# Seven half-size products for a pair of up-projection tiles in an encoder's gated MLP

## The chip, the cores and the metric

The kernel runs on one core of one Trainium2 chip. The metric is the device time of one execution in microseconds (us). The core has a matrix engine (PE, TensorE), a vector engine (DVE), a scalar or activation engine (ACT), a general engine (POOL, GpSimd), and a queue engine (SP) that here only issues transfers. SBUF is the on-chip working memory that all of them read; PSUM holds matmul results, which PE writes and DVE and ACT read. The engines run their own instruction lists strictly in order and wait for each other through semaphores.

## The reference: a two-layer encoder, and its gated MLP

`x` has 512 rows of 1024 features. Each of the two layers applies a three-branch mixer (windowed attention, dense attention, spatial gating), a cross-attention into 256 memory rows, and a gated MLP, each followed by a residual and a layer norm. The change touches the MLP:

```python
def conv_ffn(x, w_up, conv_k, conv_b, w_down):
    S = x.shape[1]
    h = x @ w_up                                  # 512 x 1024 times 1024 x 5632
    r = CONV_W // 2
    hp = jnp.pad(h, ((0, 0), (r, r), (0, 0)))
    h = sum(hp[:, j:j + S] * conv_k[j] for j in range(CONV_W)) + conv_b
    a, b = jnp.split(h, 2, axis=-1)
    return (jax.nn.gelu(a, approximate=False) * b) @ w_down   # 2816 -> 1024
```

The up-projection gives 5632 features, 44 tiles of 128. Tile j (of a) and tile 22 + j (of b) make pair j; a convolution of width 3 along the rows, a GELU and a product turn a pair into tile j of g, and g times `w_down` follows.

## The kernel before

**Numbers.** Every fp32 operand is split into a high part, rounded to the matrix engine's fp32r type by ACT (`split_hi`, L127), and a low part, the rest, by DVE (`split_lo`, L132; a few weight tiles name POOL instead). A product is three matmuls (`mm3`, L138 to L140): high by high, high by low, low by high, added in PSUM.

**Weights.** All weights stream from HBM in chunks of 128 x 1024. `Weights.load` sends a chunk into one of two `raw` tiles; `Weights.split` makes the tile `w` (high and low) in one of six slots. `pump` splits the next chunk as soon as the step that used a slot last has been written, so the splits run up to six chunks ahead.

**Order.** `layer` appends `Step`s to a list, and a scheduler places each step's instructions on the engines by its own timeline. Only SP's order is written out by hand.

**The MLP.** When the layer norm of a row block is done, `xT_step` transposes it on PE and splits it into `xT` (features on partitions; high and low). Pairs 0 and 1 are computed in halves of 256 rows (`up_half_step`), the first halves before the last row blocks have arrived. Then `up_step(j, part)` runs for pairs 2 to 21 and both parts: 8 blocks of 128 input features by three matmuls of 128 x 512, 24 matmuls to a step, into an `acc` bank. `up_post` then does the convolution, straight from that bank (`conv`: an ACT instruction into `cv`, L124, and two SCALAR_TENSOR_TENSOR on DVE, L856 and L858), GELU on ACT for part 0, and for part 1 the product on POOL (L870) and the split of `g` on ACT and DVE. The down-projection follows: 11 `down_k_step`s for each half of the output columns (24 matmuls to a step), the last four chunks of the second half taken row block by row block in `down_t_step`.

Of the kernel before, what the change touches and what calls it, by code (L numbers as in the profile page):

```python
# [16 lines left out]
P = 128  # L17
# [56 lines left out]
def encoder_kernel(ctx: ExitStack, tc: tile.TileContext, x_in, xt_in, mem_in, w_in, pp_in, ln_in, cln_in, ws_in, co_in, out):  # L74
# [66 lines left out]


    class Weights:
        def __init__(self):
            self.order, self.pos, self.last = [], {}, []
            self.raw, self.tiles = {}, {}
            self.nl = self.ns = 0

        def plan(self, steps):
            for i, st in enumerate(steps):  # L150
                for key in st.chunks:
                    if key not in self.pos:
                        self.pos[key] = len(self.order)
                        self.order.append(key)
                        self.last.append(i)
                    else:
                        self.last[self.pos[key]] = i

        def load(self):
            j = self.nl  # L160
            r = wpool.tile([P, 1024], F32, tag="raw", name="raw", bufs=N_RAW)
            l, kind, c = self.order[j]
            nc.sync.dma_start(out=r, in_=w_in[l * NCH + CHUNK_ID[kind, c]])
            self.raw[j] = r
            self.nl += 1

        def split(self):
            j = self.ns
            while self.nl <= j:
                self.load()  # L170
            t = wpool.tile([P, 2, 1024], F32R, tag="w", name="w")
            r = self.raw.pop(j)
            split_hi(t[:, 0, :], r)
            l, kind, c = self.order[j]
            split_lo(t[:, 1, :], r, t[:, 0, :], eng=nc.gpsimd if (kind, c) in POOL_LO else nc.vector)
            self.tiles[j] = t
            self.ns += 1

        def pump(self, step):
            while self.ns < len(self.order) and (self.ns < N_WSLOT or self.last[self.ns - N_WSLOT] <= step):  # L180
                self.split()
            while self.nl < len(self.order) and self.nl < self.ns + N_RAW:
                self.load()

        def get(self, key, kk, n):
# [32 lines left out]

    def xT_step(t):
# [65 lines left out]
    def layer(l):  # L285
# [555 lines left out]

        def g_slot(j):
            if j % 4 == 0 and j < 20:
                R["g", j // 4] = big_tile([P, 4, 2, S], F32R, "g")
            elif j == 20:
                R["g", 5] = kv_p.tile([P, 2, 2, S], F32R, tag="k", name="g5")
            return g_view(j)

        def g_view(j):
            return R["g", j // 4][:, j % 4]  # L850

# [10 lines left out]
        def up_post(j, part, ps):  # L862
# [4 lines left out]
            else:  # L867
                c = conv(NPAIR + j, ps)
                ca = R.pop(("ca", j))
                nc.gpsimd.tensor_tensor(out=c, in0=ca, in1=c, op=ALU.mult)  # L870
# [4 lines left out]
        def up_step(j, part):  # L875
            key = K("up", part * NPAIR + j)

            def fn():
                ps = acc_tile()
                proj_fm(ps, key)  # L880
                pump()
                up_post(j, part, ps)
            return Step(fn, [key])

# [13 lines left out]
        def down_mm(half, c, t, ps):  # L898
            w = W.get(K("down", half * 11 + c), 2, 512)
            sl = slice(t * P, (t + 1) * P)  # L900
            for j in range(2):
                k = 2 * c + j
                g = g_view(k)
                mm3(ps, g[:, 0, sl], g[:, 1, sl], w[:, 0, j, :], w[:, 1, j, :], k == 0, k == 2 * 11 - 1)
# [330 lines left out]
```

## Time and profile before

| | |
|---|---|
| runs, us | 1821.01, 1822.25, 1822.78; median 1822.25 |
| profiled execution, us | 1821.99 |
| its span, us (first to last instruction) | 1820.2 |
| granted TensorE clock, mean | 0.994 |
| busy, share of the span | PE 98%, PE weight load 83%, DVE 58%, ACT 42%, POOL 17% |
| HBM traffic | 96 GB/s over the span |
| up-projection of layer 0, pairs 2 to 21 | about 572 to 789 us of the span |

Times in the profile are us from the span's start. A group's row gives the line, engine, operation, the names written and read, the shape, the count, then busy time and mean ns of one, then the engine's idle time ahead of them and what ended it. A timeline's row gives start, duration, engine, line and operation; where neighbours are merged ("x2") the duration is that of all of them together. Matmuls are pipelined, so the distance between the starts of two neighbours, and not the duration of one, is what a matmul costs in a stream.

### The profile page before, as it was taken

To read this page: it belongs to the slowest core of one execution; us is meant where nothing else is said; L and a number is where in the kernel's file an instruction comes from. 1 tells how busy PE (TensorE), PEld (TensorE's weight loads), DVE (VectorE), ACT (ScalarE), POOL (GpSimd) and SP (SyncE) were. 2 spreads that over 40 slices of the span, in tenths; PEclk is the share of its full clock that TensorE was granted. 3 is DMA by queue.
4 is the path that set the end of the run, shared out by engine and by line. 5 is a ranking of instruction groups with operands and counts; after the bars stand their busy time and mean duration, and the time that the engine had idled before them with its cause. 6 is when DMAs were issued, how large, how long until landed. Compare 5 with 4: busy or idle time off the path is not lost.

```text
span 1820.2 us, 23541 instructions
## 1 busy us (share of the span) xinstructions
PE 1789.6 (98%) x9064; PEld 1518.3 (83%) x9064; DVE 1064.8 (58%) x1728; ACT 755.7 (42%) x1274; POOL 317.2 (17%) x320
## 2 busy tenths in 40 slices
PE   8999999999999999999999999999999999999998
PEld 6888988878979888888888888888789788888886
DVE  6566856557676555543466568565576755555334
ACT  4346645532444444431133565455325344444210
POOL 1112422221131111100011124331201311111000
PEclk9999999999999999999999999999999999999999
DMA  6221221232422322332233222212334222232331
GB/s 220 91 84 64 82 93 58 74 126 93 161 70 93 102 95 93 104 115 95 91 133 106 80 70 84 79 59 82 130 105 136 82 89 97 93 104 93 107 102 46
DMA packets 51232, 176.60 MB, mean 97 GB/s; under 512 B 5680, under 2 KB 6192, under 8 KB 50864
## 3 DMA queue, kind: packets, MB, share of 16 engines
q1 hardware_dynamic: 44784, 158.86, 26.4%
q10 hardware_dynamic: 6336, 16.23, 2.6%
q8 instruction: 72, 1.18, 0.3%
q14 instruction: 40, 0.33, 0.1%
HBM read 170.87 MB, written 4.19 MB: 96 GB/s over the span
## 4 chain that ended last, share of the span: by engine, by line
PE 97%; DVE 1%; ACT 1%; DMA 0%; issue 0%; DVEq 0%; SPq 0%
PE acc L138 26%; PE acc L139 26%; PE acc L140 25%; PE s L567 2%; PE pv L604 1%; PE t L590 1%; PE s L139 1%; PE s L138 1%; PE s L140 1%; PE t L139 1%; PE t L138 1%; PE t L140 1%; PE pv L139 1%; PE pv L549 1%; PE s L483 1%; PE pv L138 1%
## 5 line engine op out<-in xcount | busy, mean ns | idle before, releaser
L132 DVE TENSOR_TENSOR w<-raw,w 128x1024 fp32r<-128x1024 f32 x284 | 354.5, 1249 | 438.5 <-ACT w L127 437.7
L127 ACT ACTIVATE w<-raw 128x1024 fp32r<-128x1024 f32 x292 | 309.2, 1059 | 481.7 <-PE acc L140 259.2
L138 PE MATMUL acc<-xT,w 128*128 128x512 f32 (+1 forms) x1216 | 457.5, 378 | 4.2 <-DVE x L234 4.2
L140 PE MATMUL acc<-xT,w 128*128 128x512 f32 (+1 forms) x1216 | 459.2, 378 | 0.0
L139 PE MATMUL acc<-xT,w 128*128 128x512 f32 (+1 forms) x1216 | 457.4, 377 | 0.0
L138 PEld LDWEIGHTS acc<-xT,w 128*128 128x128 f32 x1216 | 228.6, 189 | 44.2 <-DVE x L234 4.6
L139 PEld LDWEIGHTS acc<-xT,w 128*128 128x128 f32 x1216 | 229.6, 189 | 40.0
L140 PEld LDWEIGHTS acc<-xT,w 128*128 128x128 f32 x1216 | 229.5, 189 | 39.4
L138 PE MATMUL acc<-w,xT 128*128 128x512 f32 (+1 forms) x384 | 137.1, 359 | 7.1 <-ACT w L127 7.1
L139 PE MATMUL acc<-w,xT 128*128 128x512 f32 (+1 forms) x384 | 137.6, 358 | 1.2 <-DVE w L132 1.2
L140 PE MATMUL acc<-w,xT 128*128 128x512 f32 (+1 forms) x384 | 137.2, 357 | 0.0
L870 POOL TENSOR_TENSOR cv<-cv 128x512 f32<-128x512 f32 x44 | 57.0, 1296 | 431.9 <-DVE cv L858 389.1
L199 POOL TENSOR_TENSOR rs<-ve,mhalf 128x1 f32<-128x1 f32 x32 | 30.2, 943 | 421.6 <-DVE ve L244 371.2
L138 PEld LDWEIGHTS acc<-w,xT 128*128 128x128 f32 x384 | 73.0, 190 | 17.0 <-ACT w L127 7.3
L139 PEld LDWEIGHTS acc<-w,xT 128*128 128x128 f32 x384 | 73.0, 190 | 12.2 <-DVE w L132 2.0
L140 PEld LDWEIGHTS acc<-w,xT 128*128 128x128 f32 x384 | 73.1, 190 | 9.6
L502 POOL TENSOR_SCALAR ring<-ring,rsm 128x256 f32<-128x256 f32 (+1 forms) x64 | 43.9, 698 | 183.6 <-DVE rsm L500 107.0
L569 DVE TENSOR_REDUCE nm<-s 128x1 f32<-128x512 f32 x64 | 43.9, 689 | 52.0 <-PE s L567 51.4
L124 ACT ACTIVATE ring<-s,nm 128x512 f32<-128x512 f32 x64 | 44.0, 688 | 68.3 <-PE t L590 44.6
L655 POOL TENSOR_TENSOR mg<-mg,ring 128x512 f32<-128x512 f32 x32 | 47.8, 1495 | 138.6 <-DVE ring L654 111.1
L576 POOL TENSOR_SCALAR ring<-ring,rsm 128x512 f32<-128x512 f32 x64 | 45.9, 731 | 127.7 <-DVE rsm L574 127.7
L124 ACT ACTIVATE cv<-acc,pp 128x512 f32<-128x512 f32 x86 | 65.4, 761 | 1.6 <-PE acc L140 1.6
(237 smaller groups left out, 3303.5 us busy)
## 6 DMA issues: line engine op xcount, KB each, us to landing
raw<-in_w_dram SPq DMA_DIRECT2D x292, 512.0 KB, 3.4
lngb<-in_ln_dram ACTq DMA_DIRECT2D x16, 256.0 KB, 4.4
xraw<-in_xt_dram SPq DMA_DIRECT2D x4, 512.0 KB, 4.8
memr<-in_mem_dram ACTq DMA_DIRECT2D x2, 1024.0 KB, 4.7
x<-in_x_dram ACTq DMA_DIRECT2D x4, 512.0 KB, 5.8
x_keep<-x ACTq DMA_DIRECT2D x4, 512.0 KB, 2.6
x<-x_keep ACTq DMA_DIRECT2D x4, 512.0 KB, 7.7
out_dram<-x SPq DMA_DIRECT2D x8, 256.0 KB, 2.0
```

Of the source, the lines that this page charges most:

```text
L124: return nc.scalar.activation(out, in_, func, **kw)
L127: nc.scalar.activation(out, in_, AF.Copy, scale=scale)
L132: eng.tensor_tensor(out=out, in0=in_, in1=hi.bitcast(F32), op=ALU.subtract)
L138: nc.tensor.matmul(ps, lhsT=lh, rhs=rh, start=first, stop=False)
L139: nc.tensor.matmul(ps, lhsT=lh, rhs=rl, start=False, stop=False)
L140: nc.tensor.matmul(ps, lhsT=ll, rhs=rh, start=False, stop=last)
L502: nc.gpsimd.tensor_scalar(out=pr_t[qi], in0=pr_t[qi], scalar1=rs[:, qi:qi + 1], scalar2=0.0, op0=ALU.mult, op1=ALU.add)
L567: nc.tensor.matmul(ps, lhsT=R["Q"][:, h, q * P:(q + 1) * P], rhs=R["Kt"][:, kv * 2 + hl, :], start=hl == 0, stop=hl == 1)
L569: nc.vector.tensor_reduce(out=nm[:, qi:qi + 1], in_=ps, axis=AX.X, op=ALU.max, negate=True)
L576: nc.gpsimd.tensor_scalar(out=pr_t[qi], in0=pr_t[qi], scalar1=rs[:, qi:qi + 1], scalar2=0.0, op0=ALU.mult, op1=ALU.add)
L655: nc.gpsimd.tensor_tensor(out=mg, in0=mg, in1=tg, op=ALU.add)
L870: nc.gpsimd.tensor_tensor(out=c, in0=ca, in1=c, op=ALU.mult)
```

## The change

Pair j, for j from 2 to 21, is now computed by `up7_steps`. The 512 x 1024 input is cut into four blocks, A11 (rows 0 to 255, first 512 features), A12 (the same rows, last 512 features), A21 and A22 (rows 256 to 511); the pair's two weight tiles are cut into B11 and B21 (tile j, the first and last 512 input features) and B12 and B22 (tile 22 + j). Winograd's form of Strassen's method needs seven block products, each of 4 blocks of 128 features by three matmuls of 128 x 256, in place of eight. Two of the seven share the first of four steps (`s0`), two the second (`s1`), two the third (`s2`) and one the last (`s3`).

The sums of input blocks are made once to a layer (`sums_step`): four subtractions or additions on POOL of 128 x 1024, split by ACT and DVE into `S31` and `S24`. For that, `xT_step` also writes the unsplit transposed block (`xf`) by one more ACT copy for each of its two halves. The sums of weight blocks are made for every pair in `split_sums`: four additions of 128 x 512 on POOL, with their results split in four parts ("us" chunks, parts 0 to 3, of 1024, 1024, 1024 and 512 columns) on ACT and DVE. The seven products are put together into a new SBUF tile `h7` by three ACT copies and five DVE additions or subtractions of 128 x 256; `up_post` then runs from `h7` and no longer from PSUM. The split of `g` moves from `up_post` into the first half of the down-projection (`gs_make`), for which `g` is kept unsplit. There are five `w` slots in place of six and four `raw` tiles in place of two. The down-projection uses other PSUM banks.

```diff
-N_WSLOT = 6
-N_RAW = 2
+N_WSLOT = 5
+N_RAW = 4
...
+        def split_sums(self, t, l, c):
+            j, i = divmod(c, US_PARTS)
+            ra, rb = self.raw.get((l, "up", j)), self.raw.get((l, "up", NPAIR + j))
+            lo, hi = slice(0, 512), slice(512, 1024)
+            if i == 0:
+                split_hi(t[:, 0, :], ra)
+                split_lo(t[:, 1, :], ra, t[:, 0, :])
+            elif i == 1:
+                u = kv_p.tile([P, 512], F32, tag="k", name="usum")
+                nc.gpsimd.tensor_tensor(out=u, in0=ra[:, lo], in1=rb[:, lo], op=ALU.add)
+                nc.gpsimd.tensor_tensor(out=rb[:, lo], in0=rb[:, lo], in1=rb[:, hi], op=ALU.add)
+                for sl, r in ((lo, rb[:, lo]), (hi, u)):
+                    split_hi(t[:, 0, sl], r)
+                    split_lo(t[:, 1, sl], r, t[:, 0, sl])
+            elif i == 2:
+                nc.gpsimd.tensor_tensor(out=ra[:, lo], in0=ra[:, lo], in1=rb[:, lo], op=ALU.add)
+                nc.gpsimd.tensor_tensor(out=ra[:, hi], in0=ra[:, hi], in1=ra[:, lo], op=ALU.add)
+                split_hi(t[:, 0, :], ra)
+                split_lo(t[:, 1, :], ra, t[:, 0, :])
+            else:
+                split_hi(t[:, 0, lo], rb[:, hi])
+                split_lo(t[:, 1, lo], rb[:, hi], t[:, 0, lo])
...
                 evac_T(xT[:, t, 0, 4 * i:4 * i + 4, :], xT[:, t, 1, 4 * i:4 * i + 4, :], pt)
+                if plain is not None:
+                    act(plain()[:, 4 * i:4 * i + 4, t * P:(t + 1) * P], pt, AF.Copy)
...
+        def gs_make(k):
+            g, v = g_view(k), gs_view(k)
+            split_hi(v[:, 0, :], g)
+            split_lo(v[:, 1, :], g, v[:, 0, :])
...
-                nc.gpsimd.tensor_tensor(out=c, in0=ca, in1=c, op=ALU.mult)
-                g = g_slot(j)
-                split_hi(g[:, 0, :], c)
-                split_lo(g[:, 1, :], c, g[:, 0, :])
+                nc.gpsimd.tensor_tensor(out=g_view(j), in0=ca, in1=c, op=ALU.mult)
...
+        def sums_step():
...
+                nc.gpsimd.tensor_tensor(out=a22, in0=a21, in1=a22, op=ALU.subtract)
+                nc.gpsimd.tensor_tensor(out=a21, in0=a11, in1=a21, op=ALU.subtract)
+                put(R["S31"][:, 0], a21)
+                put(R["S31"][:, 1], a22)
+                nc.gpsimd.tensor_tensor(out=a11, in0=a22, in1=a11, op=ALU.subtract)
+                put(R["S24"][:, 0], a11)
+                nc.gpsimd.tensor_tensor(out=a12, in0=a12, in1=a11, op=ALU.add)
+                put(R["S24"][:, 1], a12)
...
+            def s1():
+                cd, h = R["p7", j][1], R["h7", j]
+                product(cd[:, lo], 1, 0, summed("S31", 0), True, False)
+                product(cd[:, hi], 1, 1, summed("S31", 1), False, True)
+                act(h[:, 1, hi], cd[:, lo], AF.Copy)
+                nc.vector.tensor_tensor(out=h[:, 1, hi], in0=cd[:, hi], in1=h[:, 1, hi], op=ALU.subtract)
+                pump()
...
+            def s3():
+                (ab, cd), h = R.pop(("p7", j)), R.pop(("h7", j))
+                product(cd[:, hi], 3, 0, summed("S24", 1), False, True)
+                nc.vector.tensor_tensor(out=h[:, 0, hi], in0=cd[:, lo], in1=h[:, 1, lo], op=ALU.add)
+                nc.vector.tensor_tensor(out=h[:, 1, lo], in0=cd[:, hi], in1=h[:, 1, lo], op=ALU.subtract)
+                pump()
+                up_post(j, 0, h[:, 0])
+                up_post(j, 1, h[:, 1])
...
         for j in range(2, NPAIR):
-            for part in range(2):
-                st(up_step(j, part))
+            for s7 in up7_steps(j):
+                st(s7)
+        add(lambda: [gs_make(k) for k in range(2)])
```

How the change moves instructions shows on DVE and POOL. DVE in the middle of the up-projection before: the seven instructions of one pair (`w` is a weight tile's low part, `cv` the convolution, `g` the low part of g).

```order
L132 TENSOR_TENSOR w_5356<-raw_5287,w_5356 128x1024
L856 SCALAR_TENSOR_TENSOR cv_5361<-acc_5331,pp_94,cv_5361 128x511
L858 SCALAR_TENSOR_TENSOR cv_5361<-acc_5331,pp_94,cv_5361 128x511
L132 TENSOR_TENSOR w_5393<-raw_5324,w_5393 128x1024
L132 TENSOR_TENSOR g_5151<-cv_5361,g_5151 128x512
L856 SCALAR_TENSOR_TENSOR cv_5398<-acc_5368,pp_94,cv_5398 128x511
L858 SCALAR_TENSOR_TENSOR cv_5398<-acc_5368,pp_94,cv_5398 128x511
```

The convolution reads `acc`, a PSUM bank, and `cv`; the weight splits lie between. DVE at the same place now: twelve of the fourteen instructions to a pair, one behind the other (L1019 and one more `w` of 1024 columns stand just ahead of them). `t` and `acc` are PSUM banks; `h7`, `raw`, `usum`, `cv` and `w` lie in SBUF.

```order
L1020 TENSOR_TENSOR h7_5629<-t_5628,h7_5629 128x256
L134 TENSOR_TENSOR w_5784<-raw_5598,w_5784 128x512
L134 TENSOR_TENSOR w_5784<-usum_5785,w_5784 128x512
L926 SCALAR_TENSOR_TENSOR cv_5745<-h7_5629,pp_94,cv_5745 128x511
L926 SCALAR_TENSOR_TENSOR cv_5750<-h7_5629,pp_94,cv_5750 128x511
L1005 TENSOR_TENSOR h7_5757<-t_5756,h7_5757 128x256
L928 SCALAR_TENSOR_TENSOR cv_5745<-h7_5629,pp_94,cv_5745 128x511
L928 SCALAR_TENSOR_TENSOR cv_5750<-h7_5629,pp_94,cv_5750 128x511
L1013 TENSOR_TENSOR h7_5757<-h7_5757 128x256
L134 TENSOR_TENSOR w_5818<-raw_5567,w_5818 128x1024
L134 TENSOR_TENSOR w_5851<-raw_5598,w_5851 128x512
L997 TENSOR_TENSOR h7_5885<-acc_5883,h7_5885 128x256
```

The convolution's first operand is now `h7`. The split of `g` is gone from here; three splits of 512 columns and five additions of 256 columns have come in. POOL at this place had one instruction to a pair before, the product L870. Now it has five, in this order:

```order
L215 TENSOR_TENSOR usum_5785<-raw_5567,raw_5598 128x512
L216 TENSOR_TENSOR raw_5598<-raw_5598 128x512
L940 TENSOR_TENSOR g_5175<-cv_5617,cv_5622 128x512
L221 TENSOR_TENSOR raw_5567<-raw_5567,raw_5598 128x512
L222 TENSOR_TENSOR raw_5567<-raw_5567 128x512
```

L940 is the old product; L215 to L222 are the sums of weight blocks, all with both operands in SBUF.

More of the change, by code (lines that the diff above doesn't have):

```diff
@@ L168, in split @@
             j = self.ns
-            while self.nl <= j:
-                self.load()
+            key = self.order[j]
+            for k in raws_of(key):
+                while k not in self.raw:
+                    self.load()
             t = wpool.tile([P, 2, 1024], F32R, tag="w", name="w")
[L172 to L175, printed above, removed]
+            l, kind, c = key
+            if kind == "us":
+                self.split_sums(t, l, c)
+            else:
+                r = self.raw[key]
+                split_hi(t[:, 0, :], r)
+                split_lo(t[:, 1, :], r, t[:, 0, :], eng=nc.gpsimd if (kind, c) in POOL_LO else nc.vector)
+            for k in last_raws(key):
+                del self.raw[k]
+                self.freed += 1
             self.tiles[j] = t
             self.ns += 1
+        def split_sums(self, t, l, c):
+            j, i = divmod(c, US_PARTS)
+            ra, rb = self.raw.get((l, "up", j)), self.raw.get((l, "up", NPAIR + j))
[15 more added lines that the diff above has]
+                split_lo(t[:, 1, :], ra, t[:, 0, :])
+            else:
+                split_hi(t[:, 0, lo], rb[:, hi])
+                split_lo(t[:, 1, lo], rb[:, hi], t[:, 0, lo])
         def pump(self, step):
@@ L181, in pump, with ahead @@
                 self.split()
-            while self.nl < len(self.order) and self.nl < self.ns + N_RAW:
+            while self.nl < len(self.raw_order) and self.nl < self.freed + self.ahead():
                 self.load()
+        def ahead(self):
+            return N_RAW if self.raw_order[self.nl][1] == "up" else N_PLAIN
         def get(self, key, kk, n):
@@ new lines, in up7_steps, with key, plain, summed @@
+        def up7_steps(j):
+            def key(i):
+                return K("us", j * US_PARTS + i)
+            def plain(sh, kh):
+                return lambda s, k: xT[:, 2 * sh:2 * sh + 2, s, 4 * kh + k, :]
+            def summed(nm, i):
+                return lambda s, k: R[nm][:, i, s, k, :]
+            def product(o, i, part, x, first, last):
+                w = W.get(key(i), KD, P)
+                f = dict(skip_group_check=True)
+                for k in range(4):
+                    wh, wl = w[:, 0, 4 * part + k, :], w[:, 1, 4 * part + k, :]
+                    nc.tensor.matmul(o, lhsT=wh, rhs=x(0, k), start=first and k == 0, stop=False, **f)
+                    nc.tensor.matmul(o, lhsT=wh, rhs=x(1, k), start=False, stop=False, **f)
+                    nc.tensor.matmul(o, lhsT=wl, rhs=x(0, k), start=False, stop=last and k == 3, **f)
+            lo, hi = slice(0, 256), slice(256, 512)
+            def s0():
+                R["p7", j] = acc_tile(), t_tile().rearrange("p a b -> p (a b)")
+                R["h7", j] = kv_p.tile([P, 2, S], F32, tag="v", name="h7", bufs=2)
+                ab, h = R["p7", j][0], R["h7", j]
+                product(ab[:, lo], 0, 0, plain(0, 0), True, False)
+                product(ab[:, hi], 0, 1, plain(0, 1), False, True)
+                act(h[:, 0, lo], ab[:, lo], AF.Copy)
+                nc.vector.tensor_tensor(out=h[:, 0, lo], in0=ab[:, hi], in1=h[:, 0, lo], op=ALU.add)
+                pump()
+            def s1():
[5 more added lines that the diff above has]
+                pump()
+            def s2():
+                (ab, cd), h = R["p7", j], R["h7", j]
+                product(ab[:, lo], 2, 0, summed("S24", 0), False, True)
+                product(cd[:, lo], 2, 1, plain(1, 1), False, False)
+                act(h[:, 1, lo], ab[:, lo], AF.Copy)
+                nc.vector.tensor_tensor(out=h[:, 1, hi], in0=h[:, 1, hi], in1=h[:, 1, lo], op=ALU.subtract)
+                pump()
[4 more added lines that the diff above has]
+                nc.vector.tensor_tensor(out=h[:, 1, lo], in0=cd[:, hi], in1=h[:, 1, lo], op=ALU.subtract)
+                pump()
+                up_post(j, 0, h[:, 0])
+                up_post(j, 1, h[:, 1])
+            return [Step(fn, [key(i)]) for i, fn in enumerate((s0, s1, s2, s3))]
```

85 lines of the change are left out of this document (59 added, 26 removed).

## The prediction

> **What bounds the kernel now.** I read the page's busy shares first, then the chain of waits, then busy time by stage, then the distance between matmuls.
>
> ```profile
> PE 1789.6 (98%) x9064; PEld 1518.3 (83%) x9064; DVE 1064.8 (58%) x1728; ACT 755.7 (42%) x1274; POOL 317.2 (17%) x320
> PE 97%; DVE 1%; ACT 1%; DMA 0%; issue 0%; DVEq 0%; SPq 0%
> core 0: us, PE busy (x) PEld busy (x) DVE busy (x) ACT busy (x) POOL busy (x), PEclk, DMA share, GB/s
> 572.00:789.00 217.00, 216.98 (x958) 179.65 (x958) 119.92 (x143) 93.48 (x123) 27.22 (x21) 1.00 0.30 99
> ```
>
> PE is 97% of the chain that ends last. The last row is the up-projection of pairs 2 to 21 in layer 0: PE never pauses in 217 us at the full clock, while DVE works 120 us of it and POOL 27. So there fewer PE cycles are worth their full time, as long as the other engines keep up.
>
> What a matmul costs is the distance between starts. First two of 128 x 512 from this stage, then two of 128 x 256 from the half steps of pairs 0 and 1:
>
> ```profile
> 600.07 0.39 PE L138 MATMUL acc<-xT,w 128*128 128x512 f32 x1
> 600.30 0.39 PE L139 MATMUL acc<-xT,w 128*128 128x512 f32 x1
> ...
> 621.38 0.39 PE L139 MATMUL acc<-xT,w 128*128 128x512 f32 x1
> ```
>
> ```profile
> 562.44 0.28 PE L140 MATMUL acc<-xT,w 128*128 128x256 f32 x1
> 562.56 0.28 PE L138 MATMUL acc<-xT,w 128*128 128x256 f32 x1
> ...
> 571.44 0.28 PE L140 MATMUL acc<-xT,w 128*128 128x256 f32 x1
> ```
>
> From 600.30 to 621.38 lie 93 of them: 0.2267 us each. From 562.44 to 571.44 lie 75: 0.120 us each, 6% over half of 0.2267.
>
> **The change, part by part.**
>
> *PE.* A pair had 48 matmuls of 512 columns: 48 x 0.2267 = 10.88 us. It gets 7 products x 4 blocks x 3 = 84 of 256: 84 x 0.120 = 10.08 us. PE alone gains 0.80 us a pair, 32 us over the 40 pairs.
>
> *DVE, POOL and ACT for a pair.* Durations from the stage's groups, and for 256 columns from the whole run's:
>
> ```profile
> L132 DVE TENSOR_TENSOR w<-raw,w 128x1024 fp32r<-128x1024 f32 x34 | 41.7, 1226 | 82.6 <-ACT w L127 82.6
> L127 ACT ACTIVATE w<-raw 128x1024 fp32r<-128x1024 f32 x33 | 35.0, 1061 | 65.1 <-PE acc L140 65.0
> L856 DVE SCALAR_TENSOR_TENSOR cv<-acc,pp,cv 128x511 f32<-128x511 f32 x34 | 25.3, 743 | 0.0
> L124 ACT ACTIVATE cv<-acc,pp 128x512 f32<-128x512 f32 x33 | 25.1, 760 | 0.0
> L858 DVE SCALAR_TENSOR_TENSOR cv<-acc,pp,cv 128x511 f32<-128x511 f32 x33 | 24.8, 750 | 1.1
> L870 POOL TENSOR_TENSOR cv<-cv 128x512 f32<-128x512 f32 x16 | 20.7, 1296 | 151.9 <-DVE cv L858 151.9
> L132 DVE TENSOR_TENSOR g<-cv,g 128x512 fp32r<-128x512 f32 x17 | 11.6, 683 | 0.0
> L124 ACT ACTIVATE cv<-cv 128x512 f32<-128x512 f32 x17 | 10.7, 632 | 37.5 <-DVE cv L858 37.5
> L127 ACT ACTIVATE g<-cv 128x512 fp32r<-128x512 f32 x17 | 10.4, 614 | 0.0
> ```
>
> ```profile
> L132 DVE TENSOR_TENSOR mkv<-acc,mkv 128x256 fp32r<-128x256 f32 x8 | 3.2, 416 | 0.0
> L127 ACT ACTIVATE mkv<-acc 128x256 fp32r<-128x256 f32 x8 | 3.0, 380 | 4.4 <-PE acc L140 4.4
> L132 POOL TENSOR_TENSOR w<-raw,w 128x1024 fp32r<-128x1024 f32 x8 | 20.2, 2535 | 4.0 <-ACT w L127 4.0
> ```
>
> DVE now: two weight splits of 1024 columns (2 x 1.226 = 2.45), three of 512 (3 x 0.683 = 2.05), four convolution instructions (4 x 0.747 = 2.99), five additions of 256 (5 x 0.416 = 2.08): 9.57 us. Before it was 2 x 1.226 + 2.99 + 0.683 = 6.12. POOL: five of 512, 5 x 1.296 = 6.48, before 1.30. ACT: 2 x 1.061 + 3 x 0.614 + 2 x 0.760 + 0.632 + 3 x 0.380 = 7.26. Taken one by one, all fit under PE's 10.08, DVE with 0.5 us to spare.
>
> *But DVE and POOL do not work side by side.* These rows show it:
>
> ```profile
> 376.87 3.52 POOL L655 TENSOR_TENSOR mg<-mg,ring 128x512 f32<-128x512 f32 x2 [10.56 <-DVE ring L654]
> 376.89 0.69 DVE L654 SCALAR_TENSOR_TENSOR ring<-ring,acc 128x512 f32<-128x512 f32 x1 [0.17 <-PE acc L140]
> 377.98 1.26 DVE L132 TENSOR_TENSOR w<-raw,w 128x1024 fp32r<-128x1024 f32 x1 [0.40 <-ACT w L127]
> 378.12 2.28 POOL L655 TENSOR_TENSOR mg<-mg,ring 128x512 f32<-128x512 f32 x1
> ```
>
> ```profile
> 533.92 1.40 DVE L248 SCALAR_TENSOR_TENSOR x<-x,mv,lngb 128x512 f32<-128x512 f32 x2
> ...
> 540.02 2.36 POOL L132 TENSOR_TENSOR w<-raw,w 128x1024 fp32r<-128x1024 f32 x1 [0.49 <-ACT w L127]
> 540.43 3.17 DVE L248 SCALAR_TENSOR_TENSOR x<-x,mv,lngb 128x512 f32<-128x512 f32 x2
> ```
>
> ```profile
> 1312.67 1.30 POOL L655 TENSOR_TENSOR mg<-mg,ring 128x512 f32<-128x512 f32 x1 [0.64 <-DVE ring L654]
> 1312.73 1.78 DVE L134 SCALAR_TENSOR_TENSOR ml<-mg,mh 128x512 fp32r<-128x512 f32 x1 [0.20 <-ACT mh L127]
> ```
>
> At 378.12 POOL's addition meets a weight split on DVE that ends at 379.24; POOL takes 2.28 us and ends 1.16 after it. At 540.43 two DVE instructions that take 1.40 elsewhere take 3.17 behind a POOL split that ends at 542.38. At 1312.73 one that takes 0.69 takes 1.78. In each case both tensor operands of the DVE instruction lie in SBUF. The one at 376.89, with an operand in PSUM, ran its usual 0.69 beside POOL. So a DVE instruction with two SBUF operands and a POOL addition take turns, whole instruction by whole instruction.
>
> The Trainium skill, page "SBUF — State Buffer", section "Who interferes with whom", says the same: such a DVE instruction gets its second input through a read port shared with GpSimd, the later of the two is blocked fully, and one with at most one SBUF input doesn't contend. It speaks against this change, and the rows agree with it: 1.78 for 0.69, and 0.69 for 0.69.
>
> Today this costs the stage nothing: POOL's one product falls into a gap (151.9 us idle ahead of it). Now DVE's turn-taking work for a pair is 2.45 + 2.05 + 2.99 (the convolution reads `h7` in SBUF, no longer PSUM) + 0.416 (L1013) = 7.91 us, with 1.66 us of PSUM-fed additions beside, and POOL's is 6.48. The sum that must go one after the other is 14.39 us, against PE's 10.08.
>
> Bounds. Low: neighbours on DVE overlap a little, and POOL's 1.30 cost the instruction at 1312.73 only 1.78 - 0.69 = 1.09, some 1.15 with the 0.06 of its head start. Taking 0.08 from each of ten DVE instructions (row 644.20 below: it ends at 645.43, the next starts at 645.35), 7.1 + 5 x 1.15 = 12.85. High: nothing overlaps, not even the PSUM-fed additions: 9.57 + 6.48 = 16.05. I take 14.0, a little under the plain sum, since DVE's list will seldom run empty.
>
> ```profile
> 644.20 1.23 DVE L132 TENSOR_TENSOR w<-raw,w 128x1024 fp32r<-128x1024 f32 x1 [2.77 <-ACT w L127]
> 645.35 0.68 DVE L132 TENSOR_TENSOR g<-cv,g 128x512 fp32r<-128x512 f32 x1
> ```
>
> Can the rest follow at 14.0? Weight parts are split four to five ahead of PE, ACT has 7.26 us to do, and POOL's sums for the next pair stand right behind this pair's. So no wait should add to the turns; but PE will wait in every pair, for a weight part from DVE or for L1005, behind which the third and last step's accumulation into the `t` bank stands. A pair costs 14.0 - 10.88 = 3.12 us more: 20 x 3.12 = 62.4 us a layer.
>
> *Sums of the input blocks.* Four POOL instructions of 1024 columns (4 x 2.535 = 10.1) and four DVE splits (4 x 1.226 = 4.9) take turns: 15.0 us, then the products of pairs 0 and 1 (2.6). Beside them PE has the second halves of pairs 0 and 1, 96 x 0.120 = 11.5 us. I take +6 us a layer; 0 if pair sums made early fill the gap, 15 if nothing is covered.
>
> *The extra copies in the transposes*: eight ACT copies of about 0.6 us a layer, most of them beside PE's first halves; +1, between 0 and 4.8.
>
> *Moved g split.* 44 splits of 0.683 on DVE go to the down-projection, two to a step of 24 x 0.2267 = 5.44 us, where DVE has one weight split of 1.23: 2.6 of 5.44, hidden, and POOL is idle there. At the turn to it, the last pair's third weight part stands behind four such splits on ACT and DVE: 4 x 0.61 + 1.06 + 1.23 = 4.7 us against PE's second step of 24 x 0.120 = 2.9. +1, between 0 and 5.
>
> *Five slots.* Where four chunks are live at once, one and not two are split ahead. The first slot comes free a quarter step (1.36 us) into the last user, its split takes 1.06 + 1.23, so it is ready at 3.7 us, and wanted at 5.44 + 1.36 = 6.8. I cost it at nothing; without that cover 2.3 us at each of some eight such turns a layer. Raw loads: two to a pair (1 MB in 14 us), under the 99 GB/s that the stage moves now.
>
> *Sum*: 62.4 + 6 + 1 + 1 = 70.4 us a layer, 140.8 for both. The profiled execution took 1821.99 us (span 1820.2 and 1.8 around it), 0.3 under the runs' median: 1821.99 + 140.8 = 1963 us.
>
> **The rivals.**
>
> *A: the turns do not bind, PE does (faster).* If DVE's and POOL's work overlapped in this stage after all, PE's 10.08 would stand: -32 us, +4 for copies and the turn to down: 1794 us. For it: each engine alone fits (9.57, 6.48, 7.26). Against it: the three collisions quoted, each at full length, and even then DVE at 95% in strict order would have to lose under 0.5 us to waits.
>
> *B: no turns, but DVE's list binds (slower, little).* DVE's 9.57 and two waits a pair behind ACT, such as the 0.76 us of L124 between L1020 and the convolution: 9.57 + 1.5 = 11.1 a pair, +9 us over 40 pairs, with +16 for the other terms 1847.
>
> *C: turns with no overlap at all, and the same order elsewhere.* 16.05 a pair: 20 x 5.17 = 103.4 a layer, +8: 1822 + 223 = 2045 us. For it: both lists are strict, so a POOL instruction late by a turn delays ACT's split of its sum and then DVE. Against it: those sums stand a good half pair ahead of their use.
>
> *D: the change does not save its eighth.* PE's list holds 84 matmuls of 256 to a pair, so the count is as said; only the 0.120 could be off. At 0.13 the pair is 10.92, still under 14.0: no change of the time.
>
> **How the numbers follow.** My forecast has 0.77, C 0.10, B 0.05, A 0.08; D moves nothing. The forecast's own bounds are 12.85 and 14.8 a pair: 2 x (20 x 1.97) + 0 = +79 to 2 x (20 x 3.9 + 12) = +180, 1901 to 2002 us. Reaching to C for the rest of the 8 in 10: 1895 to 2035. A difference over 0.2% (3.6 us) can be told from none. Faster is A and a little: 0.09; same 0.02 (a B that costs nothing); slower 0.89.
>
> **What would show it.** In the profile after: the up stage of layer 0 about 280 us long with PE busy some 70 to 75% of it, DVE and POOL nearly full (POOL's busy time holds its waits); mean durations of L926 and L928 and of the 512-column `w` splits well over 0.75 and 0.68, POOL's L215 to L222 over 1.30; L997, L1005, L1019 and L1020 (PSUM-fed) at 0.42; 256-column matmuls 0.120 us apart where PE runs; PE's waits ended by DVE. The other stages unchanged within 1%. I am wrong if PE stays over 95% busy there, or if DVE's instructions with two SBUF operands keep their old durations beside POOL.

## The result, and the profile after

The changed kernel takes 1917.97 us (median of 4 runs, 1917.62 to 1918.73) against 1822.0 us for the kernel before (4 runs): a ratio of 1.0528, with an interval of 1.0509 to 1.0546. It is 96 us slower. The forecast was 1963 us, with a range of 1895 to 2035.

The busy line of the page and the first line of its chain of waits, after:

```profile
PE 1798.0 (94%) x10504; PEld 1584.2 (83%) x10504; DVE 1381.0 (72%) x2056; ACT 876.7 (46%) x1538; POOL 604.5 (32%) x488
PE 69%; DVE 23%; issue 4%; ACT 2%; POOL 1%; DMA 0%; DVEq 0%; ACTq 0%; SPq 0%; POOLq 0%
```

PE had 97% of the chain and now has 69%; DVE has gone from 1% to 23%. POOL's busy time has nearly doubled, from 317.2 to 604.5 us. Busy time by stretch, for the up-projection of layer 0 and for the 18 pairs between its first and its last (span, then busy us and instructions of PE, PEld, DVE, ACT, POOL, then the granted clock, the DMA share and GB/s):

```profile
572.00:840.00 268.00, 227.09 (x1712) 218.46 (x1711) 266.20 (x296) 145.42 (x238) 161.88 (x97) 0.96 0.28 87
590.63:820.65 230.02, 197.47 (x1515) 190.70 (x1513) 228.26 (x250) 120.05 (x198) 146.87 (x90) 0.96 0.27 83
```

DVE works 228.26 of 230.02 us there: it is the engine that never pauses now. How long a pair takes is read from the same row. At 590.63 the 85th of the stage's 1680 matmuls starts and at 820.65 the 1597th, and 18 x 84 matmuls lie between (the row also counts neighbours that reach over its ends): 230.02 / 18 = 12.78 us a pair, against 10.88 before and 14.0 in the forecast. Single pairs take between 10.4 and 15.5 us, so a shorter stretch gives another mean; the 12.97 and 12.66 in the expectations below are such readings. Over 40 pairs the 1.90 us more are 76 us. The other 20 us, 10 a layer, lie elsewhere.

The groups of DVE and POOL between 600 and 830 us (count, busy us, mean ns of one, idle time ahead and its releasers):

```profile
L926 DVE SCALAR_TENSOR_TENSOR cv<-h,pp,cv 128x511 f32<-128x511 f32 x36 | 45.9, 1282 | 0.0
L134 DVE TENSOR_TENSOR w<-raw,w 128x512 fp32r<-128x512 f32 x35 | 44.5, 1270 | 0.0
L134 DVE TENSOR_TENSOR w<-usum,w 128x512 fp32r<-128x512 f32 x18 | 30.8, 1713 | 0.0
L1020 DVE TENSOR_TENSOR h<-t,h 128x256 f32<-128x256 f32 x18 | 7.4, 414 | 0.1
```

```profile
L222 POOL TENSOR_TENSOR raw<-raw 128x512 f32<-128x512 f32 x18 | 29.2, 1620 | 1.4
L221 POOL TENSOR_TENSOR raw<-raw 128x512 f32<-128x512 f32 x17 | 24.6, 1449 | 25.4 <-DVE w L134 25.4
```

The first three groups of DVE, with two operands in SBUF, are 0.5 to 1.0 us longer than the 0.75 and 0.68 that these instructions took before. L928 grew less, to 1.08, and the splits of 1024 columns hardly, to 1.26 from 1.23, so the blocking falls on some places of the list more than on others. L1020, with an operand in PSUM, takes 0.414, the same as the 0.416 it was costed at. A piece of the timeline shows each collision (start, duration):

```profile
648.97 1.29 POOL L221 TENSOR_TENSOR raw<-raw 128x512 f32<-128x512 f32 x1 [3.30 <-DVE w L134]
649.08 1.74 DVE L134 TENSOR_TENSOR w<-raw,w 128x512 fp32r<-128x512 f32 x1
650.34 1.62 POOL L222 TENSOR_TENSOR raw<-raw 128x512 f32<-128x512 f32 x1
650.74 1.78 DVE L134 TENSOR_TENSOR w<-usum,w 128x512 fp32r<-128x512 f32 x1
652.44 0.41 DVE L1020 TENSOR_TENSOR h<-t,h 128x256 f32<-128x256 f32 x1
652.60 1.28 POOL L215 TENSOR_TENSOR usum<-raw 128x512 f32<-128x512 f32 x1 [0.63 <-DVE w L134]
652.77 1.65 DVE L926 SCALAR_TENSOR_TENSOR cv<-h,pp,cv 128x511 f32<-128x511 f32 x1
```

L221 starts at 648.97 and ends at 650.26; DVE's split, issued at 649.08, ends at 650.82, 0.56 us after it, about one undisturbed split (0.68). At 650.34 POOL comes behind the split that runs, and takes 1.62 us; the next split in turn takes 1.78. L215 runs its usual 1.28 while L1020 is still on DVE. These are the turns of the forecast, one instruction after the other.

PE's longest waits after (releaser, us in total, times, longest):

```profile
PE t L984 <- DVE h L1005: 32.3, 26, 2.9
PE acc L984 <- DVE h L997: 23.7, 16, 2.4
PE t L985 <- DVE S L134: 10.1, 2, 5.0
PE pv L141 <- DVE xT L134: 8.1, 2, 4.0
```

The first two come in the pairs. The third comes once a layer, inside the first pair, and the fourth once a layer ahead of all pairs; they are the beginning of the other 20 us.

### The profile page after: what moved, and what is told of

Same layout as the page of the kernel before. It is cut to its first block, busy times and chain, and to the rows that moved or that the text cites. A ratio compares the mean times of both kernels' runs of the same rounds, so it can differ in the third digit from the quotient of the medians.

```text
span 1915.9 us, 27375 instructions
## 1 busy us (share of the span) xinstructions
PE 1798.0 (94%) x10504; PEld 1584.2 (83%) x10504; DVE 1381.0 (72%) x2056; ACT 876.7 (46%) x1538; POOL 604.5 (32%) x488
## 4 chain that ended last, share of the span: by engine, by line
PE 69%; DVE 23%; issue 4%; ACT 2%; POOL 1%; DMA 0%; DVEq 0%; ACTq 0%; SPq 0%; POOLq 0%
PE acc L140 16%; PE acc L141 16%; PE acc L142 16%; DVE w L134 11%; DVE cv L926 4%; DVE cv L928 3%; PE pv L659 2%; PE s L622 2%; PE t L645 1%; ACT w L129 1%; PE s L141 1%; PE s L140 1%; PE s L142 1%; PE pv L604 1%; PE s L538 1%
## 5 line engine op out<-in xcount | busy, mean ns | idle before, releaser
L134 DVE TENSOR_TENSOR w<-raw,w 128x1024 fp32r<-128x1024 f32 x364 | 473.8, 1309 | 201.9 <-ACT w L129 197.2
L129 ACT ACTIVATE w<-raw 128x1024 fp32r<-128x1024 f32 x372 | 355.1, 963 | 349.4 <-PE acc L142 233.2
L140 PE MATMUL acc<-xT,w 128*128 128x512 f32 (+1 forms) x576 | 209.7, 367 | 0.3 <-DVE x L289 0.2
L142 PE MATMUL acc<-xT,w 128*128 128x512 f32 (+1 forms) x576 | 209.7, 365 | 0.0
L141 PE MATMUL acc<-xT,w 128*128 128x512 f32 (+1 forms) x576 | 208.9, 363 | 0.0
L140 PE MATMUL acc<-w,xT 128*128 128x512 f32 (+1 forms) x432 | 155.8, 362 | 7.0 <-ACT w L129 6.5
L142 PE MATMUL acc<-w,xT 128*128 128x512 f32 (+1 forms) x432 | 156.4, 363 | 0.0
L141 PE MATMUL acc<-w,xT 128*128 128x512 f32 (+1 forms) x432 | 155.2, 361 | 0.5 <-DVE w L134 0.5
L985 PE MATMUL t<-S,w 128*128 128x256 f32 x480 | 138.6, 290 | 10.1 <-DVE S L134 10.1
L984 PE MATMUL t<-S,w 128*128 128x256 f32 x480 | 139.4, 290 | 4.4 <-DVE h L1020 3.7
L940 POOL TENSOR_TENSOR g<-cv 128x512 f32<-128x512 f32 x44 | 86.9, 1974 | 160.7 <-DVE cv L928 138.0
L986 PE MATMUL t<-S,w 128*128 128x256 f32 x480 | 136.6, 289 | 0.5 <-DVE w L134 0.5
L142 PEld LDWEIGHTS acc<-xT,w 128*128 128x128 f32 x576 | 109.6, 190 | 15.0
L141 PEld LDWEIGHTS acc<-xT,w 128*128 128x128 f32 x576 | 109.6, 190 | 14.7
L140 PEld LDWEIGHTS acc<-xT,w 128*128 128x128 f32 x576 | 109.2, 191 | 15.0 <-DVE x L289 0.9
L126 ACT ACTIVATE cv<-h,pp 128x512 f32<-128x512 f32 x80 | 64.8, 812 | 97.3 <-DVE h L1020 69.7
L985 PEld LDWEIGHTS t<-S,w 128*128 128x128 f32 x480 | 95.2, 198 | 10.5 <-DVE S L134 10.5
L986 PE MATMUL acc<-xT,w 128*128 128x256 f32 x320 | 94.9, 296 | 6.6 <-DVE w L134 6.6
L984 PEld LDWEIGHTS t<-S,w 128*128 128x128 f32 x480 | 95.4, 199 | 6.2 <-issue 5.2
L984 PE MATMUL acc<-xT,w 128*128 128x256 f32 x320 | 94.5, 295 | 4.4 <-ACT w L129 4.4
```

Of the source, the lines that this page charges most:

```text
L126: return nc.scalar.activation(out, in_, func, **kw)
L129: nc.scalar.activation(out, in_, AF.Copy, scale=scale)
L134: eng.tensor_tensor(out=out, in0=in_, in1=hi.bitcast(F32), op=ALU.subtract)
L140: nc.tensor.matmul(ps, lhsT=lh, rhs=rh, start=first, stop=False)
L141: nc.tensor.matmul(ps, lhsT=lh, rhs=rl, start=False, stop=False)
L142: nc.tensor.matmul(ps, lhsT=ll, rhs=rh, start=False, stop=last)
```

## The experiments

All are made from the changed kernel. Times are medians; ratios are to the kernel before on the same chip.

### What makes a pair 12.8 us: three runs

**No weight sums.** POOL's four instructions for a pair are left out.

```diff
-                nc.gpsimd.tensor_tensor(out=u, in0=ra[:, lo], in1=rb[:, lo], op=ALU.add)
-                nc.gpsimd.tensor_tensor(out=rb[:, lo], in0=rb[:, lo], in1=rb[:, hi], op=ALU.add)
+                u = rb[:, hi]
...
-                nc.gpsimd.tensor_tensor(out=ra[:, lo], in0=ra[:, lo], in1=rb[:, lo], op=ALU.add)
-                nc.gpsimd.tensor_tensor(out=ra[:, hi], in0=ra[:, hi], in1=ra[:, lo], op=ALU.add)
```

> The change, with POOL's four weight sums a pair left out (the raw weight halves are split and multiplied in their place, so the products are of other numbers); PE, DVE and ACT have the instructions of the change. Turns (my theory: a DVE instruction with two SBUF operands and a POOL instruction go one after the other): POOL keeps 1.3 us a pair, DVE needs about 8.8 to 9.6 of its own, so PE's 10.08 binds again, 10.1 to 10.5 us a pair in place of 12.97: 1918 - 40 x 2.65 = about 1810 us, and L926, L928 and the 512-column weight splits back at 0.75 and 0.68. DVE's own list is the bound (rival): no change, about 1918. POOL's sums come late for the splits that need them (rival): also about 1810, but L926 and L928 would not have been long by POOL's doing, so their mean would stay over 1.0.

Measured: 1814.83 us, ratio 0.9961 [0.9945, 0.9976]. The 18 pairs between the first and the last again, and two groups of DVE (L922 is L926 here):

```profile
591.96:773.40 181.44, 181.44 (x1514) 181.44 (x1513) 155.37 (x251) 124.43 (x204) 28.65 (x17) 1.00 0.34 105
L134 DVE TENSOR_TENSOR w<-raw,w 128x512 fp32r<-128x512 f32 x53 | 36.4, 709 | 3.8 <-ACT w L129 3.5
L922 DVE SCALAR_TENSOR_TENSOR cv<-h,pp,cv 128x511 f32<-128x511 f32 x36 | 26.5, 743 | 0.0
```

A pair takes 181.44 / 18 = 10.08 us, PE never pauses, and DVE's instructions are back at 0.71 and 0.74. DVE does the same instructions as in the changed kernel, in 155.37 / 18 = 8.63 us a pair; there it was busy for 228.26 / 18 = 12.68. So POOL's four instructions, which DVE does not even issue, cost DVE 4.05 us a pair, 1.01 each.

**The weight sums on DVE.** The same four lines with `nc.vector` for `nc.gpsimd`.

> The change, with the four weight sums a pair made by DVE and not by POOL; the same result. DVE gets 4 x 0.683 = 2.7 us more to do a pair. Turns: POOL's four sums (about 1.1 us of DVE's time each, 4.4) go and 2.7 less overlap come in, so a pair falls from 12.97 to about 11.5 to 12.0 and the kernel to 1860 to 1885 us, although the busiest engine is given more work. DVE's own list is the bound (rival): a pair rises by 2.4 to 2.7 and the kernel to 2015 to 2025 us. POOL's lateness (rival): 1860 to 1885 too, but then the next run does nothing.

Measured: 1878.77 us, ratio 1.0314 [1.0297, 1.0331].

```profile
592.57:802.15 209.58, 186.10 (x1514) 182.41 (x1513) 206.02 (x322) 121.39 (x204) 30.45 (x17) 1.00 0.27 93
L222 DVE TENSOR_TENSOR raw<-raw 128x512 f32<-128x512 f32 x16 | 10.9, 681 | 0.0
```

The full engine was given four more instructions a pair and the kernel became 39 us faster: 209.58 / 18 = 11.64 us a pair. On DVE a sum takes 0.68 us; on POOL it took 1.0 us from DVE all the same. 8.63 + 4 x 0.68 = 11.35, and DVE is busy 206.02 / 18 = 11.45 us a pair, so DVE's own list is what sets the pair now.

**The convolution from PSUM.** One operand of L926 and L928 is moved from SBUF to a PSUM bank.

```diff
-                up_post(j, 0, h[:, 0])
-                up_post(j, 1, h[:, 1])
+                up_post(j, 0, ab)
+                up_post(j, 1, ab)
```

> The change, but the convolution of both tiles of a pair reads the PSUM bank of the first products and not the SBUF tile with the combined ones (the convolution is of other numbers; the combinations are still made). Every engine has the same instructions and the same columns; only one operand of four DVE instructions a pair lies in PSUM. Turns: those 2.99 us no longer exclude POOL; what must go in turn falls from 7.91 + 6.48 to 4.92 + 6.48, a pair from 12.97 to about 11 to 12, the kernel to 1840 to 1880 us, with L926 and L928 back near 0.75. DVE's own list, or POOL's lateness (rivals): no change, 1910 to 1920 us.

Measured: 1889.65 us, ratio 1.0371 [1.035, 1.0392], some 10 us over the upper end.

```profile
L134 DVE TENSOR_TENSOR w<-raw,w 128x1024 fp32r<-128x1024 f32 x30 | 49.2, 1640 | 0.0
L926 DVE SCALAR_TENSOR_TENSOR cv<-acc,pp,cv 128x511 f32<-128x511 f32 x31 | 22.7, 736 | 0.0
L1013 DVE TENSOR_TENSOR h<-h 128x256 f32<-128x256 f32 x15 | 14.7, 982 | 1.1
591.37:809.21 217.84, 191.67 (x1515) 184.59 (x1513) 215.17 (x254) 118.17 (x201) 147.81 (x91) 0.99 0.26 88
```

L926 is back to 0.736 with POOL beside it: what counts is where the operands lie. But the pair only falls to 217.84 / 18 = 12.10. The weight split of 1024 columns now takes 1.640 (1.258 in the changed kernel) and L1013 0.982 (0.657): POOL's turns went to the instructions that were left. Taking a victim away removes part of the blocking; taking four of the five blockers away brought the pair back to PE's 10.08. A kernel held up only by sums that come late from POOL would have stayed at 1910 to 1920 us here.

### What the other 20 us are: seven products for fewer pairs, or for none

In these runs the plain steps of the kernel before (`up_step`) are put back for some pairs; the rest of the change stays.

```diff
+            if j % 2:
+                for part in range(2):
+                    st(up_step(j, part))
+                continue
             for s7 in up7_steps(j):
```

**Every second pair** (j = 2, 4, ..., 20 by seven products).

> Seven products for the pairs 2, 4, ... 20 alone, eight in 24 x 2 matmuls of 512 columns for 3, 5, ... 21 as before (convolution from PSUM there); the same result. Turns: two neighbours have 12.97 + about 5.5 us of DVE and POOL's turns, 18.5, against PE's 10.08 + 10.88 = 20.96, so PE binds again: 20 pairs of seven products save 0.80 each, 16 us, less some 3 us a layer at the start and the end: 1808 to 1816 us, faster than before by 0.4 to 0.8%. DVE's own list: the same figures, as DVE has room in both; it does not tell the two apart. If the front and the turn to the down-projection cost more than the saving: 1822 to 1835.

Measured: 1831.14 us, ratio 1.0050 [1.0035, 1.0065]. PE was busy 130.00 of 130 us in the middle of the stage, with two pairs in (774.65 - 606.49) / 8 = 21.02 us between starts of PE's matmuls, 0.74 less than two old ones. So the turns were paid for out of DVE's free time in the plain pairs, as expected. Yet the kernel was slower than before: a cost outside the pairs took the gain. PE's waits:

```profile
PE t L985 <- DVE S L134: 11.5, 2, 5.7
PE pv L141 <- DVE xT L134: 8.3, 2, 4.2
```

**Two plain pairs first** (`if j < 4`): more time for the sums of the input blocks before they are needed.

> The change, with pairs 2 and 3 computed by eight products as before and seven products from pair 4 on; the same result. The runs so far split the 96 us into 40 x (12.66 - 10.88) = 71 us of pairs and 24.5 us of the rest, most of it a stop of PE for the split input sums S31 (5.0 us a layer here, 5.7 with the pairs at PE's rate) and the lowered clock behind it. If the stop is only too little PE work beside the sums, two plain pairs (21.8 us of PE work) hide it: 1918 - 4 x 1.78 - 2 x 5.0 to 6.5 = 1897 to 1901 us, and no wait for S. If the rest is not at the front: 1918 - 7 = 1911 us.

Measured: 1910.18 us, ratio 1.0485 [1.0466, 1.0504]. The wait for S was gone, and another of its kind stood in its place:

```profile
PE acc L140 <- DVE cv L928: 16.8, 2, 8.5
```

The time is the 1911 us that was expected if the rest is not at the front, but the waits are there. So it is not that the sums are needed early. Something in front of the pairs stops PE once a layer, for a sum or for an `acc` bank, whichever comes first.

**Alternate from pair 4, six slots and two raw tiles** (`if j % 2 or j < 4`, `N_WSLOT = 6`, `N_RAW = 2`).

> Seven products for the pairs 4, 6, ... 20 alone, eight for the others; six weight slots and two raw tiles as before the change; the same result. PE binds: 18 x 0.80 = 14.4 us saved; the rest, 25 us with every second pair from pair 2 on, less 11 to 13 for S31 that is now hidden, less up to 3 if the five slots cost the front: 1822 - 14.4 + 9 to 14 = 1817 to 1822 us. By the turns alone (no cost at the front beside S31) 1817; if two raw tiles hold back the seven-product pairs, over 1825.

Measured: 1827.22 us, ratio 1.0029 [1.0018, 1.0041].

```profile
PE acc L140 <- DVE cv L928: 13.0, 2, 6.5
PE pv L141 <- DVE xT L134: 1.6, 2, 0.8
```

The wait for xT is back at its 1.6 us of before, with the extra copies still there: the change from six slots and two raw tiles to five and four made it 8.3, not the copies (slots and raw tiles were not varied apart). The time is 5 us over the expected range, and over the 1825 that was to mean that two raw tiles hold the pairs back; they do not, since two pairs take 21.02 us here too. What is left is the stop of 6.5 us a layer.

**Two of three** (`if j % 3 == 0 or j < 4`, five slots).

> Seven products for the pairs 4, 5, 7, 8, 10, 11, ... 19, 20, eight for 2, 3, 6, 9, ... 21; five slots and four raw tiles; the same result. DVE and POOL's turns for three pairs are 2 x 12.66 + about 5.5 = 30.8 us, PE 2 x 10.08 + 10.88 = 31.04: PE just binds if the turns even out over three pairs. Then 24 x 0.80 = 19.2 saved and 12 to 14 us of the rest stay: 1815 to 1818 us. If they do not even out (PE waits in the seven-product pairs for 1 to 2 us and cannot make it up): 1825 to 1850.

Measured: 1855.25 us, ratio 1.0182 [1.0168, 1.0195]. Waits in the pairs came back (14.8 us on L1005 alone): one plain pair's free time on DVE does not pay for two pairs of turns. Three pairs take 33.4 us between starts of PE's matmuls where PE needs 31.04, and the time is 5 us over the worse of the two expectations.

**No pair by seven products.** Everything else of the change is there: the extra copies, the sums of input blocks (made, not read), five slots, four raw tiles, the moved split of `g`.

> No pair by seven products: all as before, but with the extra copies in the transposes, the input sums and their splits (made, and read by nothing), five slots, four raw tiles, and the split of g in the down-projection. It gives the rest without the stop for S31: if the stop and its clock are 16 to 18 of the 24.5 us, this takes 1822 + 4 to 9 = 1826 to 1831 us. If the five slots or the moved split of g are the larger part, over 1835.

Measured: 1848.54 us, ratio 1.0147 [1.0133, 1.016]. With no product saved and no weight sum made, 26 us are lost, 17 more than expected: PE stops at the front although nothing reads the sums. From 620 us on the up stage is as before (PE 160.00 of 160 us at full clock); the loss lies ahead of it. Its timeline there, by time; `S` is the split of a sum of input blocks, `cv` the convolution that frees an `acc` bank:

```profile
567.36 2.45 DVE L134 TENSOR_TENSOR S<-xf,S 128x1024 fp32r<-128x1024 f32 x1 [4.23 <-ACT S L129]
568.80 3.27 POOL L963 TENSOR_TENSOR xf<-xf 128x1024 f32<-128x1024 f32 x1
569.73 3.43 DVE L134 TENSOR_TENSOR w<-raw,w 128x1024 fp32r<-128x1024 f32 x1
573.74 2.72 DVE L134 TENSOR_TENSOR w<-raw,w 128x1024 fp32r<-128x1024 f32 x1
576.39 0.74 DVE L928 SCALAR_TENSOR_TENSOR cv<-pv,pp,cv 128x511 f32<-128x511 f32 x1
577.20 1.28 ACT L126 ACT_TABLE_LOAD   x1 [3.14 <-DVE cv L928]
579.98 0.76 ACT L126 ACTIVATE cv<-acc,pp 128x512 f32<-128x512 f32 x1
580.86 0.77 PE L140 MATMUL acc<-xT,w 128*128 128x512 f32 x1 [6.99 <-ACT cv L126]
```

DVE stands idle 4.23 us up to the first split of a sum, and the convolutions of pairs 0 and 1 stand behind that split in the list; it takes 2.45 us, and then two weight splits of 1.23 take 3.43 and 2.72 beside POOL's sums. DVE's first L928 comes at 576.39, ACT's GELU and its next `cv` behind that, and PE stops for 6.99 us.

A new theory came from this: what costs is the place of the four splits in the lists of ACT and DVE, ahead of the convolutions. The next two runs test it.

**Late splits.** POOL's four sums stay; their splits go behind the convolutions of pairs 2 and 3.

```diff
-                put(R["S31"][:, 0], a21)
-                put(R["S31"][:, 1], a22)
...
+                R["put"] = [lambda: put(R["S31"][:, 0], a21), lambda: put(R["S31"][:, 1], a22),
+                            lambda: put(R["S24"][:, 0], a11), lambda: put(R["S24"][:, 1], a12)]
...
                     st(up_step(j, part))
+                    if j in (2, 3):
+                        st(put_step())
```

In the kernel that alternates from pair 4 with six slots:

> As e6_alternate_six_slots (seven products for pairs 4, 6, ..., 20; six slots, two raw tiles), and the splits of the four block sums S31 and S24 come after the convolutions of pairs 2 and 3 in the program instead of ahead of the second halves of pairs 0 and 1; POOL's four sums stay where they were. Theory (in the lists of ACT and DVE these splits stood ahead of the convolutions that free the `acc` banks, and waited there for POOL): the wait of acc on cv L928 (13.0 us in e6) goes, with some microseconds of low clock behind it: 1827 - 13 - 1..5 = 1809-1813, under the kernel before. Rival (PE stops there whatever the order, because DVE and POOL together have too much to do in the stage's first 50 us): 1822-1828, with another wait of 5 us or more a layer in its place.

Measured: 1815.19 us (5 runs), ratio 0.9962 [0.9949, 0.9974]: faster than the kernel before by 0.4%, and by 5.4% than the changed one. In DVE's and PE's timelines:

```profile
571.39 0.74 DVE L928 SCALAR_TENSOR_TENSOR cv<-pv,pp,cv 128x511 f32<-128x511 f32 x1
574.25 0.74 PE L140 MATMUL acc<-xT,w 128*128 128x512 f32 x1 [2.06 <-ACT cv L126]
```

The first L928 comes 2.6 us earlier than in the same kernel with early splits (574.00 there), and the stop is 2.06 us a layer where it had been 6.5. Twelve us of time went with 8.9 us of waits. The result is 2 us above the expectation's upper end, and the stop did not go altogether.

In the kernel without any pair by seven products:

> As e8_scaffold_only (no pair by seven products; block sums made and not read; five slots, four raw tiles), with the same later place of the four splits. Theory: the wait of acc on cv L126 (14.0 us in e8) and most of the low clock behind it go: 1848.5 - 14 - 4..8 = 1827-1831; the 6.6 us that the xT wait grew by stay. Rival (the cost comes from the work itself, not from its place): within 4 us of 1848.

Measured: 1838.17 us, ratio 1.0088 [1.0075, 1.0102]: 10 us of the 26 are gone, against 18 to 22 expected. PE's waits, and two rows of DVE's timeline:

```profile
PE pv L141 <- DVE xT L134: 8.5, 2, 4.2
PE acc L140 <- DVE cv L928: 6.8, 2, 3.4
568.44 1.70 DVE L134 TENSOR_TENSOR w<-raw,w 128x1024 fp32r<-128x1024 f32 x1 [4.97 <-ACT w L129]
570.73 2.77 DVE L134 TENSOR_TENSOR w<-raw,w 128x1024 fp32r<-128x1024 f32 x1
```

The place of the splits was half of that wait of 14.0 us. DVE's idle time is not part of that half: it is 4.97 us here, now up to a weight split that waits for ACT. The other half remains with POOL's sums where they were, beside DVE's weight splits (2.77 for 1.23 in the row at 570.73); that these turns cost it was not tried by taking the sums away. The xT wait is untouched, as expected.

### Two more tries for a better kernel

**Two of three pairs, weight sums on DVE, late splits, five slots.**

> Seven products for pairs 4, 5, 7, 8, ..., 19, 20 (as e7_two_of_three, 1855), the four sums of weights on DVE instead of POOL (as e2_weight_sums_on_dve), and the splits of the block sums after pairs 2 and 3. DVE was full at 11.64 us a pair of seven products in e2 and needs about 8.7 a plain pair or less, so two and one need 32 us or less where PE needs 2 x 10.05 + 10.88 = 31: theory (what binds is DVE's list alone once POOL does not interfere): close to PE bound, 1822 - 2 x 12 x 0.83 + 2 x 12 x 0..0.5 + 6 for the xT wait = 1808-1820. Rival (collisions of DVE with POOL's remaining product, or the late order of its list, keep more than 0.5 us a pair): over 1825.

Measured: 1823.86 us (10 runs), ratio 1.0012 [1.0002, 1.0021], 4 us above the theory's range and just under the rival's.

```profile
620.00:780.00 160.00, 159.52 (x1097) 148.74 (x1096) 147.81 (x218) 89.28 (x141) 30.82 (x15) 1.00 0.33 109
PE pv L141 <- DVE xT L134: 8.3, 2, 4.3
PE acc L140 <- DVE cv L928: 8.0, 2, 4.0
```

The stage itself is PE's again, 159.52 of 160 us: with the sums on DVE, two of three pairs fit. The gain of the products, 24 x 0.80 = 19 us, is lost, most of it to the two waits at the front.

**The same with six slots and two raw tiles.**

> As e11_two_of_three_dve_sums, with six slots and two raw tiles in place of five and four. Theory (five slots are what makes the xT wait 8.3 us instead of 1.6, as e4 against e6 showed, and part of the acc wait of 8.0): 1823.9 - 6.7 - 0..4 = 1813-1817, under the kernel before. Rival (two raw tiles hold one seven-product quarter, so the loads of the next one start late where two such pairs follow each other): PE waits for weights in the up stage, over 1824.

Measured: 1851.79 us, ratio 1.016 [1.0146, 1.0174]: the rival's.

```profile
620.00:780.00 160.00, 149.13 (x1006) 137.05 (x1005) 132.15 (x192) 80.15 (x123) 30.43 (x15) 0.99 0.27 86
PE acc L140 <- ACT w L129: 17.1, 12, 6.6
```

PE waits for a weight tile twelve times where it had done so once in the run before (at the very start), and traffic falls from 109 to 86 GB/s: two raw tiles are too few where two pairs by seven products follow each other. The theory's part on the front came: the waits there fell, that for xT to 1.6 us and that behind `cv` to 4.1. Four raw tiles cost the front a slot, and two cost the pairs their loads.

## Why the prediction was right, and where it was not

**The mechanism was right.** The product count and the 0.120 us a matmul held (a PE-bound pair takes 10.08 us, as forecast), every engine's own work fitted under it (DVE's 8.63, 9.57 forecast), and the turns of DVE and POOL made the difference. The run without weight sums gives back 103 us of the time (40 x 2.70 = 108 by the pairs); the run with the sums on DVE rules out rival B, since more work on the same list made the kernel faster; C's 16.05 is far off; A's pair is what is seen once POOL's sums are gone. The signs named beforehand came: L926, L928 (1.08) and the 512-column splits long, PSUM-fed additions at 0.41, POOL's sums over 1.30 (1.45 to 1.62), DVE full, PE's waits ended by DVE. Two signs did not. POOL was to be nearly full and is busy 146.87 of 230.02 us; in between it stands idle, mostly for DVE (25.4 us ahead of L221 alone). PE's share of the stage was forecast at 70 to 75% and read 85% (227.09 of 268); 10.08 of 12.78 us make 79%, and the rest was not worked out.

**The pair was mis-sized: 12.78, not 14.0.** The step that failed is the choice "a little under the plain sum", within bounds of 12.85 and 16.05; the measurement lies just under the lower bound. The sum took each POOL instruction at its whole 1.296 us. A sum cost DVE 1.01, less than even the 1.15 of the lower bound, which had been worked out from one collision in the trace of before (1.78 for 0.69). That one collision was the better guide: it showed what POOL takes from DVE, where the duration only shows what POOL needs. The lower bound then left the PSUM-fed additions out as hidden (1.66 us) and charged 1.15 for each of five POOL instructions; measured, the additions count in DVE's 8.63, and a sum costs less, perhaps because part of it can run beside them, as L215 does at 652.60 under L1020. The two errors nearly cancel. Correcting this term alone gives 1822 + 76 + 16 = 1914.

**The front was mis-sized, and its reason was another.** The terms beside the pairs came to 8 us a layer and measured 10; where the pairs run at PE's rate it is 12 to 13 (7 us gained of 32 in the run without weight sums, 26 us lost with no pair by seven products). "+6 for the sums of the input blocks" counted DVE's and POOL's busy time against PE's; what happened is an order: in strict lists the splits that wait for POOL stood ahead of convolutions that free PSUM banks (late splits: -12 and -10 us). "Five slots: nothing" was wrong: the wait for xT went from 1.6 to 8.1 us over both layers, and six slots (with two raw tiles) took it back. I looked for the cover of five slots inside the pairs, and the cost came ahead of them, where the split of xT is awaited. "+1 for the copies" was that much or less: with six slots they left the waits as before. "+1 for the split of g and the turn to the down-projection" held roughly. For the split of g: without seven products and with late splits, the stretch from 780 to 960 us has PE busy 178.0 us against 180.0 before. For the turn: the last pair, with eight matmuls of the down-projection in it (1.8 us), is 2.5 us longer than 12.78 and those eight together (17.1 us, from 820.65 to 837.73); in the run without weight sums it is 0.8 us longer than 10.08 and the eight.

What stays open is how the 20 us divide. The waits S and xT together grew by 16.6 us in the changed kernel. Around these stops the granted clock is lower too, 0.90 from 530 to 600 us against 0.98 before; the low clock described below was not varied by itself.

## What to carry to other kernels

Before moving additions to POOL to relieve a full DVE, look for one place in the trace where the two meet: if both have their operands in SBUF, POOL's work is charged to DVE, here 1.0 us for an addition that DVE does itself in 0.68. Then put an instruction that waits for a slow engine behind, not ahead of, the ones that free banks for the fast one; in strict lists its place can cost more than its length. A saving of 7% on a stage's bound survives only as far as the other engines have free time there: alternating old and new pairs kept most of it inside the stage (0.74 of 0.80 us a pair) and 0.4% of the whole with late splits, and using it everywhere turned it into a loss of 5%.

## What the runs showed of the hardware that was not expected

A short stop of PE can cost more than its length. In the kernel with late splits, matmuls of 256 columns run 0.12 us apart up to 571.91, then PE stops for 2.06 us, and then:

```profile
574.79 0.63 PE L141 MATMUL acc<-xT,w 128*128 128x512 f32 x1
575.21 0.63 PE L142 MATMUL acc<-xT,w 128*128 128x512 f32 x1
...
577.35 0.56 PE L141 MATMUL acc<-xT,w 128*128 128x512 f32 x1
577.75 0.39 PE L142 MATMUL acc<-xT,w 128*128 128x512 f32 x1
```

The stream starts again at 574.25 (the row shown with that kernel). From 574.79 to 577.35 six intervals of 0.427 us, then 0.23 us again: eight matmuls at half speed, 8 x 0.2 = 1.6 us more for a stop of 2.06. After the 6.99 us stop in the run with no pair by seven products the spell is as long (from 580.86 to 584.41). Not every stop has one. In the changed kernel three matmuls behind a stop of 2.94 us take 0.46 us together, two of the three distances at 0.12:

```profile
784.62 0.39 PE L984 MATMUL t<-xT,w 128*128 128x256 f32 x1 [2.94 <-DVE h L1005]
785.08 0.28 PE L984 MATMUL t<-xT,w 128*128 128x256 f32 x1
```

The Trainium skill, page "TensorE: Matmul & The Clock Gate", section "What's actually happening", has the matrix clock halved after at least one idle window of about 3.4 us and restored after a busy one. The half and the length of the spell agree with the trace; the length of the stop does not, for 2.06 us was enough here, and 2.94 us was not elsewhere.
